# Hybrid MoBA/NSA decoder layer on one core: token projections in 512-column pieces, q and k heads turned in fp32 pairs, weights split up to eight tiles ahead, attention preludes polled in steps

## The chip, the cores and the metric

The kernel runs on one core of one Trainium2 chip. The time is the device time of one execution in microseconds; the runs before agree within 0.2 us. The engines are named as in the profile: PE (TensorE, the matmuls; PEld is its weight load), DVE (VectorE), ACT (ScalarE), POOL (GpSimd) and SP (SyncE, which here issues the DMAs).

## What is computed

One decoder layer on x of 512 tokens by 1024 channels, all in float32. One input projection feeds two mixers: A is a block-sparse attention of 8 heads of 64, B a three-branch attention (compressed, selected, window) of 8 query heads in 2 groups.

```python
h = rms_norm(x, norm_w); proj = h @ w_in            # 1024 -> 5912 columns
(q_a, k_a, v_a, z_a, q_b, kc, vc, ksl, vsl, kwn, vwn, gate_b, z_b, gate_m) = split(proj)
o_a = moba_mixer(rms_norm(q_a), rms_norm(k_a), v_a, bias_a)
o_b = nsa_mixer(rms_norm(q_b), rms_norm(compress(kc)), compress(vc),
                rms_norm(ksl), vsl, rms_norm(kwn), vwn, sigmoid(gate_b), bias_b)
merged = sigmoid(gate_m[:1024]) * ((o_a * silu(z_a)) @ w_branch_a) \
       + sigmoid(gate_m[1024:]) * ((o_b * silu(z_b)) @ w_branch_b)
out = x + merged @ w_out
```

At 512 tokens every block is selected, so both mixers are dense causal attention with a bias: 8 units (one per head) for A, 16 units (a head and a branch) for B.

## The kernel before

**Arithmetic.** Each fp32 operand of a matmul is split into a high and a low part in the reduced type fp32r, and a product is three matmuls: high by high, low by high, high by low (`mm3`; the issuing line of all of them is 343). Weights come from HBM as 128-row tiles of up to 560 columns (`wr`, six buffers), `Stream.split` makes `wh` (a copy on ACT, line 314, or on POOL, line 316) and `wl` (a subtraction on DVE or POOL, line 318). `Stream.take` hands out the next tiles; `ahead` splits at most four tiles ahead of the one in use.

**Projection.** Token-major pieces (`gemm_tok`, PSUM tile `pgt`) compute 128 tokens by n columns: four row tiles t, eight k each, three matmuls per k. The first piece (`gemm_first`, `pgf`) runs k outermost while x arrives. Its columns are 256: `v0`, `v1`, four `qk` pieces with two q heads and two k heads each, `qb0`, `qb1`; `kb` has 280 and `vb` 256. Channel-major pieces (`gemm_chan`, `pgc`) have the weight as the stationary side and all 512 tokens as the moving side: `kc`, `vc`, eight z gates, eight merge gates (`gmgate`).

**From projection to attention.** `norm_split` takes a row tile of four heads out of PSUM (`nraw` on ACT), squares, sums (line 617), takes the power -0.5 on POOL (`nr`, line 385), multiplies (619), applies the gain (614) and splits into high and low halves of a token tile (595, 596). `q_stack` and `k_stack` turn one head, high and low half together, by four 128x128 transposes in fp32r (`stack`, PSUM tile `pq`, line 825) and copy it out (832): `qs`, `ks`, and `kx` with the halves swapped. A unit then makes scores (`sps`, lines 893 and 894), bias and row minimum (912, DVE), exp (927, ACT), the division (931, POOL), the transposes of P in fp32 (`pt`, 940), their split (952 ACT, 954 DVE) and the product with v (`O`, 974).

**Order.** The program is written by a planner at build time. Four generators (x statistics, `attention`, `gemms`, `cmp` for the compression) yield PE work with an assumed cost, or a condition to wait for; the planner picks the generator with the least weighted time whose condition holds, and ACT, DVE and POOL steps hang on chains in a heap of assumed times. So each engine has one fixed order, and every engine runs its order strictly in turn. In `attention` the prelude of unit n+2 (the turns of its head, its bias row `T`) is advanced by one step after each score block of unit n, and what is left of it is run to its end, waits included, before unit n+1. After the last unit `x_again` forms the sums of x (`xa`, `ta`, `tb`, split into `T`, `th`, `hh`, `hl`) that the merge gates of mixer B need. Behind the z and merge gates come the branch products (`pbr`), four `gate_pair`s (`pgw`) and the output projection (`po`).

Of the kernel before, what the change touches and what calls it, by code (L numbers as in the profile page):

```python
# [19 lines left out]
D = 1024  # L20
DH = 64
# [15 lines left out]
NATT = 39  # L37
NW = 8
NRAW = 6
# [36 lines left out]
def tok_layout():  # L76

    lay, n = {}, 0
    for name, cols in tok_pieces().items():
        lay[name] = (n, KT // 2, len(cols))  # L80
        n += KT // 2
    return lay, n
# [3 lines left out]
def hybrid_kernel(ctx: ExitStack, tc: tile.TileContext, x, x0, xT, wtok, wchan, wgate, gains, w1,  # L86
# [28 lines left out]
    RES = {"g": (pg, 2), "s": (pss, 2), "t": (pst, 3), "o": (pso, 1), "sb": (sp, 3), "gmt": (sp, 3), "nraw": (sp, 4),  # L115
# [164 lines left out]
    class Stream:  # L280
# [19 lines left out]
        def split(w, upto):  # L300
            while len(w.chain) < min(upto, len(w.raws)):
# [6 lines left out]
                hi, lo = w.mk_hi()[:, :n], w.mk_lo()[:, :n]  # L308
# [133 lines left out]
    def x_rms():  # L442
# [10 lines left out]
        x_diag(c)  # L453

# [30 lines left out]
    def tok_tiles(name):  # L485
        i0, nt, n = tlay[name]
        return [(wtok[i0 + i][:, :2 * n], 2 * n) for i in range(nt)]
# [4 lines left out]
    ORDER_T = ("v0", "qk0", "qk1", "kc", "qk2", "vc", "v1", "qk3", "qb0", "kb", "vb", "za0", "za1", "qb1", "za2", "za3", "zb0", "zb1", "zb2", "zb3")  # L492
# [41 lines left out]
    for p_, c in [(p_, c) for p_ in (1, 2) for c in range(2)] + [(p_, c) for c in range(2) for p_ in (5, 6, 3, 7, 4)]:  # L534
        tiles += [(operand(p_, 2, 2 * c + i), 512) for i in range(2)]
    W = Stream(tiles, NRAW - 1, lambda: wp.tile([P, WT], F32R, name=nm("wh"), tag="whi"),
               lambda: wp.tile([P, WT], F32R, name=nm("wl"), tag="wlo"))
    W1 = Stream([(w1[kv, q], 512) for kv in range(2) for q in range(8)], 1, lambda: att("vh"), lambda: att("vl"))
# [5 lines left out]
    def gemm_tok(name, emit, tags="gggg"):  # L544
        n = tlay[name][2]
        ws = W.take(4, n)
        for t in range(NT):
            yield room(tags[t])
            ps = psum(tags[t], "pgt")
            hs = [(hh[:, k, t * P:(t + 1) * P], hl[:, k, t * P:(t + 1) * P], None) for k in range(KT)]  # L550
            i = 0
            for c in mm3(ps[:, :n], hs, ws):
                yield c
                if not callable(c):
                    i += 1
                    ahead((t + i / KT) / NT)
            with_rx(lambda t=t, ps=ps: emit(t, ps))

    def gemm_first(name, emit, tags="ggss"):

        n = tlay[name][2]
        ws = W.take(4, n)
        ps = [psum(tag, "pgf") for tag in tags]
        for k in range(KT):
            for a, b in ((0, 0), (1, 0), (0, 1)):
                yield need(f"xl{k}" if a else f"xh{k}")
                if b or not a:
                    yield need((W, b, k // 2))
                for t in range(NT):
                    nc.tensor.matmul(ps[t][:, :n], (hl if a else hh)[:, k, t * P:(t + 1) * P], ws[k][b],  # L570
# [4 lines left out]
            ahead((k + 1) / KT)  # L575

    def gemm_chan(name, emit):
# [5 lines left out]
        for c in mm3(ps, ws, [(hh[:, k, :], hl[:, k, :], None) for k in range(KT)]):  # L583
            yield c
            if not callable(c):
                i += 1
                ahead(i / KT / 2)
# [10 lines left out]
    def norm_split(ch, dst, ps, t, g0):  # L598

        b = {}  # L600

        def f0(e):
            b["raw"] = alloc("nraw", "nraw", (P, 4, DH))
            b["xn"] = sp.tile([P, 4, DH], F32, name=nm("nxn"), tag="nxn", bufs=4)
            b["ss"] = sp.tile([P, 4], F32, name=nm("nss"), tag="nss", bufs=4)
            b["r"] = sp.tile([P, 4], F32, name=nm("nr"), tag="nr", bufs=4)
            e.activation(b["raw"], ps[:, :256].rearrange("p (h d) -> p h d", h=4), AF.Copy, scale=rx[:, t:t + 1])

        def f1(e):
            if g0 == 2:  # L610
                e.tensor_mul(b["xn"], b["xn"], gn[:, g0, :].unsqueeze(1).to_broadcast([P, 4, DH]))
            else:
                x4 = b["xn"].rearrange("p (a b) d -> p a b d", a=2)
                e.tensor_mul(x4, x4, gn[:, g0:g0 + 2, :].unsqueeze(2).to_broadcast([P, 2, 2, DH]))
        ch.do({"A": 358}, f0, ps, "nraw")
        ch.do({"A": ca(256)}, lambda e: e.activation(b["xn"], b["raw"], AF.Square))
        ch.do({"D": cd(256)}, lambda e: e.reduce_sum(b["ss"], b["xn"], axis=AX.X))
        rsqrt_mean(ch, lambda: b["r"], lambda: b["ss"], DH, 4)
        ch.do(either(256), lambda e: e.tensor_mul(b["xn"], b["raw"], b["r"].unsqueeze(2).to_broadcast([P, 4, DH])))
        ch.do(either(256), f1)  # L620
        split(ch, dst, lambda: b["xn"], lambda: b["raw"])
# [7 lines left out]
    def proj_norm(name, g0, tags="gggg"):  # L629
        toks[name] = [None] * NT  # L630

        def emit(t, ps):
            toks[name][t] = att(name)
# [4 lines left out]
            norm_split(ch, hl4(toks[name][t]), ps, t, g0)  # L638
# [8 lines left out]
    def proj_v(name, first=False):  # L647
        toks[name] = [None] * NT

        def emit(t, ps):  # L650
            toks[name][t] = att(name)
            ch = Chain(now[0] + 230)
            dst, src, r = hl4(toks[name][t]), ps[:, :256].rearrange("p (h d) -> p h d", d=DH), rx[:, t:t + 1]
            ch.do({"A": 358}, lambda e: e.activation(dst[:, :, 0, :], src, AF.Copy, scale=r))
            ch.do({"D": 396}, lambda e: e.scalar_tensor_tensor(
                dst[:, :, 1, :], src, r, dst[:, :, 0, :].bitcast(F32), op0=ALU.mult, op1=ALU.subtract), ps)
            ch.mark(f"{name}.{t}")
# [163 lines left out]
    def stack(srcs):  # L821

        pt = psum("t", "pq", F32R)
        for t in range(NT):
            nc.tensor.transpose(pt[:, t * P:(t + 1) * P], srcs[t], identr)  # L825
# [8 lines left out]
    def q_stack(box, srcs):  # L834
        yield room("t")
        pt = stack(srcs)
        yield 4 * 85
        qs = att("qs")
        box.append((qs, Chain(now[0] + 230).do({"A": 478, "D": 600}, lambda e: copy_on(e, qs, pt.bitcast(F32)), pt)))

    def k_stack(box, srcs, first=None):

        yield room("t")
        pt = stack(srcs)
        yield 4 * 85
        ks = att("ks")
        kx = att("kx")
        c = Chain(now[0] + 230)
        c.do({"A": 478, "D": 600}, lambda e: copy_on(e, ks, pt.bitcast(F32)))
        c.do({"A": 478, "D": 600}, lambda e: copy_on(e, kx[0:64, :], pt[64:128, :].bitcast(F32)))  # L850
        c.do({"A": 478, "D": 600}, lambda e: copy_on(e, kx[64:128, :], pt[0:64, :].bitcast(F32)), pt)
        if first is not None:
            for i, z in enumerate((ks, kx)):
                def f(e, dst=first[:, i, :], src=z[:, :P].bitcast(F32)):
# [5 lines left out]
        box.append((ks, kx, c))  # L860
# [159 lines left out]
    def moba_units():  # L1020
        us = []
        for h in range(8):
            p, i = h // 2, h % 2
            box = {"q": [], "k": []}

            def pre(h=h, p=p, i=i, box=box):
                yield toks_of(f"qk{p}")
                yield toks_of(f"v{h // 4}")
                yield from q_stack(box["q"], heads(f"qk{p}", i))
                yield from k_stack(box["k"], heads(f"qk{p}", 2 + i))  # L1030
                yield late
# [572 lines left out]
```

## Time and profile before

| | |
|---|---|
| median of 3 runs | 471.98 us (471.87 to 472.05) |
| the profiled execution | 473.72 us, span of its instructions 471.9 us |
| PE busy | 463.5 us, 98% of the span, 3172 matmuls |
| DVE, ACT, POOL busy | 386.5, 281.1, 184.5 us |
| DMA moved | 74.40 MB, 158 GB/s in the mean |

Rows of a group view read: line, engine, operation, out<-in by the program's names, shape, count | busy us, mean ns of one | idle us of the engine before them and what ended it. A matmul's duration holds its way through the array, which overlaps the next matmul; what it costs the stream is the distance from its start to the next start. In the chain (the work that ended last, followed back) a row is the start, the length, and what ran.

### The profile page before, as it was taken

The page shows a single profiled execution, that of the slowest core. Times are in us where ns is not written, and L with a number is a line of the kernel's source. Part 1 is how long each engine was busy: PE and PEld are TensorE (multiplying, and loading weights), DVE is VectorE, ACT ScalarE, POOL GpSimd, SP SyncE. Part 2 cuts the span into 40 slices and gives each one's busy share as a digit, 9 for nine tenths or more (in the row PEclk, how much of TensorE's full clock was granted, in tenths as well). Part 3 has the DMA queues.
Part 4 walks back from the last instruction along what each step waited for, and adds up shares of the span by engine and source line. Part 5 has one row for each costly group of instructions (what it writes and reads, how often), then busy time and mean ns, then how long its engine had stood idle before and what let it go on. Part 6 is the DMA issues. An engine that isn't in the chain of part 4 may idle for free.

```text
span 471.9 us, 9247 instructions
## 1 busy us (share of the span) xinstructions
PE 463.5 (98%) x3172; PEld 424.2 (90%) x3172; DVE 386.5 (82%) x972; ACT 281.1 (60%) x683; POOL 184.5 (39%) x242
## 2 busy tenths in 40 slices
PE   9999999999999999999999999999998999999997
PEld 9999897999999889888888888888886998999996
DVE  5888899798998569898877967787499699999873
ACT  7667594487776338476777557787473554556220
POOL 0154373048666205445546327555723022202120
PEclk9999999999999999999999999999999999999999
DMA  8925234534334423165565675664996785568862
GB/s 303 269 66 191 58 80 144 149 102 128 108 105 123 116 87 91 48 178 133 160 132 156 141 202 107 179 120 148 261 275 155 264 209 167 163 197 268 248 205 69
DMA packets 41088, 74.40 MB, mean 158 GB/s; under 512 B 3984, under 2 KB 6416, under 8 KB 41040
## 3 DMA queue, kind: packets, MB, share of 16 engines
q1 hardware_dynamic: 32464, 57.02, 39.4%
q0 software_dynamic: 4352, 8.39, 10.9%
q10 hardware_dynamic: 4224, 8.39, 5.3%
q8 instruction: 25, 0.41, 0.4%
q14 instruction: 23, 0.19, 0.1%
HBM read 71.03 MB, written 19.53 MB: 192 GB/s over the span
## 4 chain that ended last, share of the span: by engine, by line
PE 80%; DVE 8%; ACT 5%; POOL 2%; DMA 2%; issue 1%; SPq 0%; POOLq 0%; DVEq 0%; ACTq 0%
PE pgc L343 18%; PE pgt L343 17%; PE pgw L343 9%; PE po L343 8%; PE pbr L343 7%; PE O L974 6%; PE pt L940 5%; PE sps L893 3%; PE sps L894 3%; DVE wl L318 2%; PE pq L825 1%; POOL P L931 1%; DMA wr<-in_w 1%; DMA x<-in_xT 1%; ACT wh L314 1%
## 5 line engine op out<-in xcount | busy, mean ns | idle before, releaser
L318 DVE TENSOR_TENSOR wl<-wr,wh 128x512 fp32r<-128x512 f32 (+1 forms) x139 | 97.3, 714 | 6.5 <-ACT wh L314 5.1
L343 PE MATMUL pgt<-wh,hh 128*128 128x256 f32 (+1 forms) x288 | 82.9, 288 | 1.6 <-DVE X L711 0.8
L343 PE MATMUL pgt<-wl,hh 128*128 128x256 f32 (+1 forms) x288 | 81.5, 283 | 0.3 <-DVE wl L318 0.2
L343 PE MATMUL pgt<-wh,hl 128*128 128x256 f32 (+1 forms) x288 | 81.2, 282 | 0.0
L314 ACT CAST wh<-wr 128x512 fp32r<-128x512 f32 (+1 forms) x98 | 59.1, 615 | 17.2 <-DMA wr<-wsum 11.7
L316 POOL TENSOR_SCALAR wh<-wr 128x512 fp32r<-128x512 f32 (+1 forms) x50 | 39.4, 795 | 76.1 <-DMA wr<-wsum 31.0
L931 POOL TENSOR_SCALAR P<-P,sst,gate 128x512 f32<-128x512 f32 (+3 forms) x56 | 40.3, 728 | 55.4 <-DVE sst L930 42.5
L912 DVE CUSTOM_DVE_ANT_0 sb<-sps,T 128x512 f32<-128x512 f32 (+3 forms) x96 | 46.0, 485 | 18.9 <-PE sps L894 17.7
L343 PE MATMUL pgc<-hh,wh 128*128 128x512 f32 x144 | 59.4, 413 | 0.0
L343 PE MATMUL pgc<-hl,wh 128*128 128x512 f32 x144 | 56.9, 395 | 0.0
L343 PE MATMUL pgc<-hh,wl 128*128 128x512 f32 x144 | 56.8, 395 | 0.0
L927 ACT ACTIVATE P<-sb,sst 128x512 f32<-128x512 f32 (+3 forms) x88 | 50.8, 578 | 9.9 <-DVE sst L912 8.9
L343 PEld LDWEIGHTS pgt<-wh,hh 128*128 128x128 f32 x288 | 54.2, 188 | 2.6 <-PE pgt L343 1.0
L343 PEld LDWEIGHTS pgt<-wl,hh 128*128 128x128 f32 x288 | 54.2, 188 | 0.7 <-DVE wl L318 0.7
L343 PEld LDWEIGHTS pgt<-wh,hl 128*128 128x128 f32 x288 | 54.2, 188 | 0.5
L952 ACT CAST ph<-pt 128x512 fp32r<-128x512 f32 (+2 forms) x72 | 33.2, 478 | 34.9 <-PE pt L940 34.0
L931 POOL TENSOR_SCALAR P<-P,sst 128x512 f32<-128x512 f32 (+3 forms) x32 | 24.8, 779 | 45.4 <-DVE sst L930 38.8
L940 PE MATMUL pt<-cst,P 128*128 128x128 f32 x232 | 40.8, 273 | 0.3 <-POOL P L931 0.2
L954 DVE TENSOR_TENSOR pl<-pt,ph 128x512 fp32r<-128x512 f32 (+2 forms) x72 | 38.4, 549 | 2.1 <-ACT ph L952 1.8
L385 POOL TENSOR_TENSOR nr<-nss,mhalf 128x4 f32<-128x4 f32 x28 | 29.7, 1062 | 24.3 <-DVE nss L384 23.8
L940 PEld LDWEIGHTS pt<-cst,P 128*128 128x128 f32 x232 | 28.9, 140 | 4.8 <-POOL P L931 1.5
L343 PEld LDWEIGHTS pgc<-hl,wh 128*128 128x128 f32 x144 | 27.0, 188 | 6.4
(267 smaller groups left out, 1278.9 us busy)
## 6 DMA issues: line engine op xcount, KB each, us to landing
wr<-in_wtok SPq DMA_DIRECT2D x36, 256.0 KB, 3.0
wr<-wsum SPq DMA_DIRECT2D x32, 256.0 KB, 3.4
wr<-in_wgate SPq DMA_DIRECT2D x28, 256.0 KB, 3.1
wr<-in_wchan SPq DMA_DIRECT2D x20, 256.0 KB, 2.8
T<-rtab SPq DMA_DIRECT2D x16, 256.0 KB, 3.9
wr<-in_w SPq DMA_DIRECT2D x16, 256.0 KB, 2.7
wsum<-in_wgate ACTq DMA_DIRECT2D x4, 1024.0 KB, 5.5
wsum<-wsum POOLq DMA_DIRECT2D x8, 512.0 KB, 6.5
```

The lines of the kernel that those rows point to most:

```text
L314: e.copy(hi, raw)
L316: e.tensor_scalar(hi, raw, 1.0, 1.0, op0=ALU.mult, op1=ALU.mult)
L318: c.do(either(n), lambda e, hi=hi, lo=lo, raw=raw: e.tensor_sub(lo, raw, hi.bitcast(F32))).mark((w, 1, i))
L343: nc.tensor.matmul(dst, sts[i][a], mvs[i][b], start=(start and i == a == b == 0), stop=(stop and i == n - 1 and b == 1), skip_group_check= ...
L385: c.do({"p": 430 + 150 * w}, lambda e: e.tensor_tensor(v(dst), v(ss), mhalf[:parts, :w], op=ALU.pow))
L912: e.tensor_tensor_reduce(z["sb"][:, :L], sps[:, :L], T[:, S - L:], scale=-1.0, scalar=3e38, op0=ALU.add, op1=ALU.min, accum_out=st[:, 0, b ...
L927: e.activation(pv(), z["sb"][:, :L], AF.Exp, bias=st[:, 0, b:b + 1], scale=-1.0, accum_out=st[:, 1, b:b + 1])
L931: c.do({"P": 315 + 0.834 * L}, lambda e: e.tensor_scalar(pv(), pv(), st[:, 2, b:b + 1], g, op0=ALU.mult, op1=ALU.mult))
L940: nc.tensor.transpose(pt[:, (b - kb) * P:(b - kb + 1) * P], u.p0 if u.p0 is not None and b == 0 else u.pb[:, POFF[b] + kb * P:POFF[b] + (k ...
L952: e.copy(z["w"][0], pt[:, :w])
L954: ch.do({"D": cd(w)}, lambda e: e.tensor_sub(z["w"][1], pt[:, :w], z["w"][0].bitcast(F32)), pt)
L974: nc.tensor.matmul(O[0][:, S - n:], v.bitcast(F32) if kb == 3 else v, w, start=(u.first and kb == 0 and i == 0), stop=(u.last and kb == 3 ...
```

## The change

- **Pieces of 512 columns.** `v0` and `v1` become `v`, the four `qk` pieces become two of four q and four k heads, `qb0` and `qb1` become `qb`. A weight tile then holds one k of 512 columns instead of two of 256; there are 40 token tiles as before. `kb` and `vb` keep their columns. `qb` and `kb` change places, and the late `qb1` moves up with `qb0`.
- **Norms on eight heads at a time,** left in fp32: no split of token tiles. The product of the q and the k gain, with the factor 0.125, is formed once in `gn` and applied to k alone, so q gets no gain step.
- **Turns in pairs.** `turn` transposes two fp32 heads at a time (128 columns); `q_pair` copies the high part of each head (ACT) and subtracts for the low part (DVE); `k_pair` writes the high part twice into `ks`, and the low part into both halves of `kx` (DVE, then an ACT copy).
- **Weights further ahead.** `more` splits up to eight tiles ahead during a token piece and during `kc` and `vc`; every second tile of a 512-column piece takes its `wh` and `wl` from the attention pool, which grows from 39 to 41 tiles; `nraw` has two buffers of twice the size.
- **Preludes in steps.** After each score block, the prelude of unit n+1, or of n+2 when that is through, is polled: a step whose condition does not hold yet is put aside. Only before a unit starts is its own prelude run to the end.
- The bias rows and the row of x's scale (`bias_rows`, `x_rows`) move from the GEMM's generator to that of the x statistics, ahead of the second piece.

```diff
-NATT = 39
+NATT = 41
+AHEAD = 8
...
-    d = {f"qk{p}": r(QA + 128 * p, 128) + r(KA_ + 128 * p, 128) for p in range(4)}
-    d.update({f"v{i}": r(VA + 256 * i, 256) for i in range(2)})
-    d.update({f"qb{i}": r(QB + 256 * i, 256) for i in range(2)})
+    d = {f"qk{g}": r(QA + 256 * g, 256) + r(KA_ + 256 * g, 256) for g in range(2)}
+    d.update(v=r(VA, 512), qb=r(QB, 512))
...
-        lay[name] = (n, KT // 2, len(cols))
+        kk = WT // len(cols)
+        lay[name] = (n, KT // kk, len(cols), kk)
...
     def gemm_tok(name, emit, tags="gggg"):
-        n = tlay[name][2]
-        ws = W.take(4, n)
+        _, nt, n, kk = tlay[name]
+        ws = []
         for t in range(NT):
...
+            for k in range(KT):
+                if not t and not k % kk:
+                    ws += W.take(1, n)
+                    W.split(W.i + min(nt - 1 - k // kk, 3))
+                h = hh[:, k, t * P:(t + 1) * P], hl[:, k, t * P:(t + 1) * P], None
+                yield from mm3(ps[:, :n], [h], [ws[k]], start=(k == 0), stop=(k == KT - 1))
+                if t:
+                    f = (t + (k + 1) / KT) / NT
+                    more(int(AHEAD * min(1, f / 0.75) + 0.5), 4 - (k // 2 if t == NT - 1 else 0))
...
-        ch.do({"A": 358}, f0, ps, "nraw")
-        ch.do({"A": ca(256)}, lambda e: e.activation(b["xn"], b["raw"], AF.Square))
-        ch.do({"D": cd(256)}, lambda e: e.reduce_sum(b["ss"], b["xn"], axis=AX.X))
-        rsqrt_mean(ch, lambda: b["r"], lambda: b["ss"], DH, 4)
-        ch.do(either(256), lambda e: e.tensor_mul(b["xn"], b["raw"], ...))
-        ch.do(either(256), f1)
-        split(ch, dst, lambda: b["xn"], lambda: b["raw"])
+        ch.do({"A": 100 + cap(n)}, f0, ps, "nraw")
+        ch.do({"A": ca(n)}, lambda e: e.activation(out, b["raw"], AF.Square))
+        ch.do({"D": cd(n)}, lambda e: e.reduce_sum(b["ss"], out, axis=AX.X))
+        rsqrt_mean(ch, lambda: b["r"], lambda: b["ss"], DH, H)
+        ch.do(either(n), lambda e: e.tensor_mul(out, b["raw"], ...), lambda: b["t"])
...
-            nc.tensor.transpose(pt[:, t * P:(t + 1) * P], srcs[t], identr)
+            nc.tensor.transpose(pt[:, t * P:(t + 1) * P], toks[name][t][:, col:col + P], ident)
...
+        for r, z in enumerate(qs):
+            c.do({"A": 478}, lambda e, r=r, z=z: e.copy(z[0:64, :], pt[64 * r:64 * r + 64, :]))
+        for r, z in enumerate(qs):
+            c.do({"D": 602}, lambda e, r=r, z=z: e.tensor_sub(z[64:128, :], pt[64 * r:64 * r + 64, :], z[0:64, :].bitcast(F32)),
+                 pt if r else None)
...
-                yield from until_cost(nxt, n)
+                for m in range(n + 1, min(n + 3, len(units))):
+                    if m not in over:
+                        yield from poll(m)
+                        break
...
-            yield from nxt
             prev = u
...
     def gemms():
-        yield from proj_v("v0", True)
-        yield from proj_norm("qk0", 0, "ttto")
-        yield from bias_rows()
-        yield from x_rows()
-        yield from proj_norm("qk1", 0)
+        yield from proj_v("v", ("v0", "v1"), True)
+        yield from proj_norm("qk0", 1, "ttto")
         yield from compress_w(0)
-        yield from proj_norm("qk2", 0)
+        yield from proj_norm("qk1", 1)
         yield from compress_w(1)
-        yield from proj_v("v1")
-        yield from proj_norm("qk3", 0)
-        yield from proj_norm("qb0", 2)
         yield from proj_norm("kb", 4)
-        yield from proj_v("vb")
+        yield from proj_norm("qb", 0)
+        yield from proj_v("vb", ("vb",))
```

What the order of the instructions makes of it, at three places. The names carry buffer numbers.

PE at the first preludes, before: the turns of head 0 (`pq_700` q, `pq_708` k) inside the third row tile of the piece `qk1`, behind `v0` and `qk0`. `identr` is the identity in fp32r.

```order
L343 MATMUL pgt_665<-wl_483,hh 128x256
L825 MATMUL pq_700<-identr,qk_455 128x128
L825 MATMUL pq_700<-identr,qk_457 128x128
L825 MATMUL pq_700<-identr,qk_511 128x128
L825 MATMUL pq_700<-identr,qk_557 128x128
L825 MATMUL pq_708<-identr,qk_455 128x128
L825 MATMUL pq_708<-identr,qk_457 128x128
L825 MATMUL pq_708<-identr,qk_511 128x128
L825 MATMUL pq_708<-identr,qk_557 128x128
L825 MATMUL pq_719<-identr,qk_455 128x128
```

The same place on PE now; `cst` is the fp32 identity.

```order
L344 MATMUL pgt_707<-wl_517,hh 128x512
L850 MATMUL pq_715<-cst,qk_503 128x128
L850 MATMUL pq_715<-cst,qk_565 128x128
L850 MATMUL pq_715<-cst,qk_616 128x128
L850 MATMUL pq_715<-cst,qk_659 128x128
L850 MATMUL pq_725<-cst,qk_503 128x128
L850 MATMUL pq_725<-cst,qk_565 128x128
L850 MATMUL pq_725<-cst,qk_616 128x128
L850 MATMUL pq_725<-cst,qk_659 128x128
L344 MATMUL pgt_707<-wh_531,hh 128x512
```

What were two stacks for one head (a third, `pq_719`, begins the next head) are two stacks for two heads. They stand inside the first row tile of the new `qk1`, behind `v`, the whole of the new `qk0` (four q and four k heads) and `kc`.

DVE at the norms of `qk0`, before: the steps of several 256-column row tiles, with the split of the finished ones (line 596).

```order
L619 TENSOR_TENSOR nxn_468<-nraw_467,nr_470 128x256
L617 TENSOR_REDUCE nss_565<-nxn_564 128x4
L614 TENSOR_TENSOR nxn_468<-nxn_468,gn 128x256
L384 TENSOR_SCALAR nss_565<-nss_565 128x4
L619 TENSOR_TENSOR nxn_473<-nraw_472,nr_475 128x256
L318 TENSOR_TENSOR wl_586<-wr_399,wh_585 128x512
L614 TENSOR_TENSOR nxn_473<-nxn_473,gn 128x256
L596 TENSOR_TENSOR qk_455<-nxn_468,qk_455 128x4x64
L619 TENSOR_TENSOR nxn_518<-nraw_517,nr_520 128x256
```

The same place on DVE now: four steps per row tile of eight heads, with weight splits of the next pieces between them.

```order
L636 TENSOR_REDUCE nss_509<-qk_503 128x8
L385 TENSOR_SCALAR nss_509<-nss_509 128x8
L319 TENSOR_TENSOR wl_554<-wr_498,wh_553 128x512
L638 TENSOR_TENSOR qk_503<-nraw_508,nr_510 128x512
L641 TENSOR_TENSOR qk_503<-qk_503,gn 128x256
L319 TENSOR_TENSOR wl_578<-wr_537,wh_577 128x512
L636 TENSOR_REDUCE nss_573<-qk_565 128x8
L385 TENSOR_SCALAR nss_573<-nss_573 128x8
L319 TENSOR_TENSOR wl_596<-wr_540,wh_595 128x512
```

The split is gone. Of the multiplications the one with the power (638) now covers eight heads, and the one with the gain (641) the 256 k columns of those alone.

DVE at the end of attention, before: `ys` takes over the last attention output, `gm_5049` is the last merge gate of the first half, and the sums of x (`ta`, `tb`) stand behind it, between the branch products (line 1347).

```order
L1003 TENSOR_TENSOR ys_4938<-O_5011,ot_5132 64x512
L318 TENSOR_TENSOR wl_5135<-wr_4795,wh_5134 128x512
L1013 TENSOR_TENSOR ys_4938<-ys_4938,zs_3843 128x512
L1206 TENSOR_TENSOR gm_5049<-pgc_5050,R 128x512
L1015 TENSOR_TENSOR yl_5146<-ys_4938,yh_5145 128x512
L1214 TENSOR_TENSOR ta_5105<-xa_5101 128x256
L318 TENSOR_TENSOR wl_5167<-wr_4841,wh_5166 128x512
L1215 TENSOR_TENSOR ta_5105<-xa_5103,ta_5105 128x256
L1347 SCALAR_TENSOR_TENSOR gm_4001<-gm_4001,pbr_5154 128x512
L1214 TENSOR_TENSOR ta_5111<-xa_5107 128x256
```

The same place on DVE now: `gm_4364` is the third last merge gate.

```order
L1037 TENSOR_TENSOR ys_4174<-O_4249,ot_4369 64x512
L319 TENSOR_TENSOR wl_4373<-wr_4019,wh_4372 128x512
L1047 TENSOR_TENSOR ys_4174<-ys_4174,zs_3464 128x512
L1049 TENSOR_TENSOR yl_4385<-ys_4174,yh_4384 128x512
L319 TENSOR_TENSOR wl_4399<-wr_4105,wh_4398 128x512
L1256 TENSOR_TENSOR ta_4340<-xa_4336 128x256
L1257 TENSOR_TENSOR ta_4340<-xa_4338,ta_4340 128x256
L1248 TENSOR_TENSOR gm_4364<-pgc_4365,R 128x512
L1256 TENSOR_TENSOR ta_4346<-xa_4342 128x256
L1268 SCALAR_TENSOR_TENSOR T_4335<-ta_4340,T_4335 128x256
```

Attention now ends three whole merge-gate products (72 matmuls of 512 columns on PE) before the branch products, where it ended in the last of them (12 matmuls before its end), and three quarters of the sums of x are made beside those products.

More of the change, by code (lines that the diff above doesn't have):

```diff
@@ L453, in x_rms @@
         x_diag(c)
+        yield from bias_rows()
+        yield from x_rows()
     def x_diag(c):
@@ L549, in gemm_tok, with more @@
             ps = psum(tags[t], "pgt")
[L550 to L556, printed above, removed]
-            with_rx(lambda t=t, ps=ps: emit(t, ps))
+            for k in range(KT):
[7 more added lines that the diff above has]
+                    more(int(AHEAD * min(1, f / 0.75) + 0.5), 4 - (k // 2 if t == NT - 1 else 0))
+            with_rx(lambda t=t, ps=ps: emit(t, ps))
+    tlay_next = ("kc", "vc")
+    def more(n, used):
+        i = W.i
+        while i < W.i + n:
+            used += i not in from_att
+            if used > NW:
+                break
+            i += 1
+        W.split(i)
     def gemm_first(name, emit, tags="ggss"):
         n = tlay[name][2]
-        ws = W.take(4, n)
         ps = [psum(tag, "pgf") for tag in tags]
         for k in range(KT):
+            w = W.take(1, n)[0]
+            W.split(W.i + 2) if k < 5 else more(k, 4)
             for a, b in ((0, 0), (1, 0), (0, 1)):
@@ L574, in gemm_first @@
                 yield cm(n) * NT
-            ahead((k + 1) / KT)
+        W.split(W.i + 4)
     def gemm_chan(name, emit):
@@ L586, in gemm_chan @@
                 i += 1
-                ahead(i / KT / 2)
+                if name in tlay_next:
+                    more(int(8 * min(1, i / KT) + 0.5), 2)
+                else:
+                    ahead(i / KT / 2)
         emit(ps)
@@ L1094, in pre0 @@
             box["pcc"] = cc
-            yield late
             yield room("T")
@@ L1145, in attention, with drain, poll @@
         pres = [p() for p, _ in units]
-        yield from pres[0]
-        yield from pres[1]
-        prev = None
-        def until_cost(g, n):
-            if n in lates:
-                return
-            for v in g:
-                if v is late:
-                    lates.add(n)
-                    return
-                yield v
-                if not callable(v):
-                    return
-        lates = set()
+        pend, over = {}, set()
+        def drain(m):
+            if m in pend:
+                yield pend.pop(m)
+            yield from pres[m]
+            over.add(m)
+        def poll(m):
+            while True:
+                v = pend.pop(m, None) or next(pres[m], None)
+                if v is None:
+                    over.add(m)
+                    return
+                if not callable(v):
+                    yield v
+                    return
+                t = v()
+                if t is None or t > now[0]:
+                    pend[m] = v
+                    return
+        prev = None
         for n in range(len(units) + 1):
             u = units[n][1] if n < len(units) else None
-            nxt = pres[n + 2] if n + 2 < len(units) else iter(())
             if u:
+                yield from drain(n)
                 yield from u.start()
```

177 lines of the change are left out of this document (95 added, 82 removed).

## The prediction

> **What bounds the kernel now.** I read first the busy table of the page and its row of the granted clock, then the shares of the chain, PE's waits, and PE beside the other engines in three stretches. "DVE" is the third group of the second row.
>
> ```profile
> span 471.9 us, 9247 instructions
> PE 463.5 (98%) x3172; PEld 424.2 (90%) x3172; DVE 386.5 (82%) x972; ACT 281.1 (60%) x683; POOL 184.5 (39%) x242
> PEclk9999999999999999999999999999999999999999
> PE 80%; DVE 8%; ACT 5%; POOL 2%; DMA 2%; issue 1%; SPq 0%; POOLq 0%; DVEq 0%; ACTq 0%
> ```
>
> PE is busy for 98% of the span at the full granted clock, and 80% of the chain runs on it. So there are two ways to gain: less work in PE's stream, and fewer holes in it. The holes that have a releaser:
>
> ```profile
> PE pbr L343 <- ACT hh L1228: 1.4, 1, 1.4
> PE pw L402 <- POOL ones L357: 0.9, 1, 0.9
> PE pgt L343 <- DVE X L711: 0.8, 1, 0.8
> PE pgt L343 <- ACT nraw L607: 0.7, 1, 0.7
> PE hps L740 <- DVE vl L318: 0.3, 1, 0.3
> PE pt L940 <- POOL P L931: 0.2, 1, 0.2
> PE pgt L343 <- DVE wl L318: 0.2, 1, 0.2
> ```
>
> Their sum is 4.5 us, 0.9 of it the start of the program. So at most 3.6 us is to be had from these waits; the rest of a gain must come from PE's own work. The second engine is DVE. In windows, with columns span; then busy (and count) of PE, PEld, DVE, ACT, POOL; clock; DMA share; GB/s:
>
> ```profile
> 60.00:70.00 10.00, 10.00 (x79) 9.61 (x78) 9.69 (x32) 9.55 (x27) 7.11 (x9) 1.00 0.24 51
> 200.00:240.00 40.00, 39.77 (x229) 34.17 (x228) 33.83 (x106) 26.96 (x76) 19.12 (x28) 1.00 0.62 158
> 340.00:366.00 26.00, 24.65 (x107) 19.65 (x106) 25.23 (x44) 14.13 (x29) 7.71 (x7) 1.00 0.81 217
> ```
>
> DVE is 97% busy from 60 to 70 us and from 340 to 366 us, 85% in the attention between. In the first PE loses nothing, in the last it does. The 1.4 us wait lies there:
>
> ```profile
> 360.47 1.51 DVE L1218 TENSOR_TENSOR tb<-ta,xa 128x256 f32<-128x256 f32 x1
> 362.07 0.62 ACT L1228 CAST T<-tb 128x512 fp32r<-128x512 f32 x1 [5.14 <-DVE tb L1218]
> 363.06 0.47 PE L343 MATMUL pbr<-yh,wh 128*128 128x512 f32 x1 [1.35 <-ACT hh L1228]
> ```
>
> The sums of x that end attention run on DVE beside the branch products, and ACT, waiting 5.14 us for one of them (`tb`), is late with the casts that stand ahead of what PE needs.
>
> **The change, part by part.**
>
> *Pieces of 512 columns.* What one matmul costs PE's stream is read from unbroken stretches of the chain:
>
> ```profile
> 148.91 4.27 PE pgt L343 x36
> 266.57 8.34 PE pgc L343 x36
> ```
>
> 36 matmuls of 256 columns take 4.27 us, 118.6 ns each; 36 of 512 take 8.34 us, 231.7 ns each. A pair of the former is 237.2 ns, so a merge saves 5.5 ns. How many there are (the others of these three parts have the same count):
>
> ```profile
> L343 PE MATMUL pgt<-wh,hh 128*128 128x256 f32 x256 | 73.4, 287 | 1.6 <-DVE X L711 0.8 <-ACT nraw L607 0.7
> L570 PE MATMUL pgf<-wh,hh 128*128 128x256 f32 x32 | 5.8, 306 | 0.0
> ```
>
> 3 x (256 + 32) = 864, of which the 96 of `vb` keep their width. 768 x 118.6 ns = 91.1 us become 384 x 231.7 ns = 89.0 us: **-2.1 us**, all of it on PE's path.
>
> The Trainium skill, page "TensorE: Matmul & The Clock Gate", section "Back-to-back issue gap", puts an isolated warm matmul of N columns at N/2.4 + 2.5 ns, a fixed part of 2.5 ns per matmul; by that the 384 merges would give 1.0 us where the rows give 2.1. Its 109.2 and 215.8 ns lie under the measured 118.6 and 231.7, so here the measurement decides.
>
> *Turns in pairs.* The transposes now:
>
> ```profile
> L825 PE MATMUL pq<-identr,qk x64: 220/245/306, 39.1 to 135.3; 128*128 128x128 f32 x64
> L825 PE MATMUL pq<-identr,qb x32: 224/246/304, 180.2 to 260.1; 128*128 128x128 f32 x32
> L825 PE MATMUL pq<-identr,kb x16: 221/246/304, 174.7 to 254.9; 128*128 128x128 f32 x16
> ```
>
> 112 in fp32r, 28 stacks of four; after, 14 stacks of four in fp32. No fp32 `pq` exists before; the nearest row is `pt`, the transposes of P, fp32 against the same identity. Both kinds in the stream, each with the matmuls behind it:
>
> ```profile
> 40.90 0.46 PE L825 MATMUL pq<-identr,qk 128*128 128x128 f32 x4
> 41.20 0.35 PE L343 MATMUL pgt<-wh,hh 128*128 128x256 f32 x1
> 41.38 0.28 PE L343 MATMUL pgt<-wh,hl 128*128 128x256 f32 x1
> ...
> 130.01 0.60 PE L940 MATMUL pt<-cst,P 128*128 128x128 f32 x4
> 130.36 0.38 PE L343 MATMUL pgt<-wh,hh 128*128 128x280 f32 x1
> 130.58 0.30 PE L343 MATMUL pgt<-wh,hl 128*128 128x280 f32 x1
> ```
>
> From the stack's start to the second matmul behind it is 0.48 us in fp32r; less 0.12 for the matmul between, 0.36 us. In fp32 it is 0.57 less 0.13 (280 columns at the rate of 118.6 ns for 256), 0.44; other `pt` stacks lie a little above, so I take 0.45. 28 x 0.36 = 10.1 us become 14 x 0.45 = 6.3 us: **-3.8 us**. The ends: at 0.36 a stack -5.0, at twice the fp32r price -0.
>
> *Norms of eight heads, no split, halves made behind the turn.* This is work of DVE and ACT. DVE's rows, the last one of a size that it gets now:
>
> ```profile
> L617 DVE TENSOR_REDUCE nss<-nxn 128x4 f32<-128x256 f32 x28 | 11.4, 410 | 0.1
> L619 DVE TENSOR_TENSOR nxn<-nraw,nr 128x256 f32<-128x256 f32 x24 | 12.0, 498 | 2.1 <-POOL nr L385 1.8
> L596 DVE TENSOR_TENSOR qk<-nxn,qk 128x256 fp32r<-128x256 f32 x13 | 5.8, 445 | 1.7 <-ACT qk L595 1.7
> L384 DVE TENSOR_SCALAR nss<-nss 128x4 f32<-128x4 f32 x28 | 5.4, 196 | 0.1
> L614 DVE TENSOR_TENSOR nxn<-nxn,gn 128x256 f32<-128x256 f32 x17 | 7.5, 442 | 0.1
> L832 DVE CAST kx<-pq 64x512 fp32r<-64x512 f32 x7 | 4.8, 687 | 0.6 <-ACT ks L832 0.3
> L1003 DVE TENSOR_TENSOR ys<-O,ot 64x512 f32<-64x512 f32 x16 | 10.9, 680 | 3.6 <-ACT ot L999 3.4
> ```
>
> By the order, DVE's part of the token splits (23 x 0.445 = 10.2 us) goes. Of the sums, 28 x 0.41 = 11.5 become 12 of twice the width, estimated at the 0.68 of `ys`, and 4 of the old: 9.8. Of the products, 24 x 0.498 = 12.0 become 11 x 0.68 + 4 x 0.498 = 9.5. New are 28 subtractions behind the turns, 28 x 0.68 = 19.0; gone are 15 copies of the old turns at the 0.687 of `kx`, 10.3, 11 of 17 gain steps, 4.9, and 12 of 28 small scalings of 0.196, 2.4. Together DVE loses some 13 us of 386. None of it is on PE's path as long as DVE keeps its lead, so I book it at nothing; the cover is the GEMM that stands between a head's turn and its first score. With that cover gone, each of the 14 pairs would hold PE by at least its two subtractions, 1.4 us, 19 us in all.
>
> *Order.* The first score now stands here:
>
> ```profile
> 43.04 0.40 PE L893 MATMUL sps<-ks,qs 128*128 128x512 f32 x1
> ```
>
> In the new order 252 matmuls of 512 columns and two stacks stand ahead of it behind the start at 5.5 us: 5.5 + 58.4 + 0.9 = 65 us. Attention begins 22 us later. It nevertheless ends earlier against the rest: behind its last PE work stood 12 matmuls of 512 columns (2.8 us) ahead of the branch products, now 72 (16.7 us). So the sums of x have 14 us more until PE needs their successors, and the wait of 1.4 us (`pbr`) goes: **-1.4 us**. The two waits of `pgt` (0.8 and 0.7) belong to pieces that no longer exist. Their kind stays: a row tile of a token piece has to be copied out before its PSUM buffer serves again. With 512 columns the row tile's matmuls last 24 x 231.7 ns = 5.6 us, so the copies have twice the time; but in `kb`, of 280 columns, two tiles are reused in a tight row behind a 512-column piece. I put 1.5 us back for such waits, as much as goes: 0.
>
> *Weights.* A tile of the new pieces serves one k, three matmuls of 512, 0.695 us, where a tile of two k served six of 256, 0.71 us, in the first row tile of a piece; in the other three no tile is needed. The pace asked of DVE at a piece's head is so the same, and what eight tiles of lead give is cover for the head. No gain, no loss; the ends are the 0.2 us of the `wl` wait going, and a hole at some of the six heads, up to 0.7 us each, the time of one tile, 4 us. The bias and x rows are moved, with the same instructions on PE: three matmuls, booked at 0; they now stand among GEMM of the first pieces. SP issues the same 222 DMAs; the bias row's comes earlier and attention's later, so no queue gets more to carry before its first user.
>
> *Sum:* -2.1 - 3.8 - 1.4 = -7.3, and with the tenths of the smaller waits -7.4 us. The profiled execution took 473.72 us, 1.74 above the median of the runs, so the difference is set against the median: 471.98 - 7.4 = **464.6 us**. What a measurement of this kernel can tell is about 0.2%, 0.9 us.
>
> **The rivals.**
>
> *The PE work goes, the waits eat part of it.* The work alone, 5.9 us, gives 466.1. If in addition the heads of the six pieces each cost up to 0.7 us (4 us) and the reuse in `kb` another, it is 470 to 471. For it: DVE at 97% where pieces follow each other (60 to 70 us), and every prelude put off makes a later lump. Against it: in that very stretch PE lost nothing. 466 to 471, **0.30**.
>
> *Slower: attention starved.* The 24 units now have to fit between 65 us and the end of attention, with fewer GEMM matmuls between their blocks. If PE, as it waits on the chain of minimum, exp and division, loses 0.3 us per unit, 24 x 0.3 = 7.2 us eat the gain; that is the point from which it decides. At 0.5 us it is 12 us and 476.6. For it: DVE is at 85% between 200 and 240 us, and the same chains pack closer. Against it: PE's wait for `P` was 0.2 us in all, and DVE has 13 us less. **0.07**.
>
> *More than that.* If every wait of the list but the start's goes, -5.9 - 3.6 = -9.5, 462.5; DVE's 13 us may also close the small holes that no row of the list names, a few us more, to 460. **0.08**.
>
> *Nothing comes of it.* The merges bring less per matmul than the rows of an unbroken stretch say, fp32 stacks cost near twice, and 1.4 us moves elsewhere: within 0.2% of before, **0.05**.
>
> *PE's rate at 512 columns.* If long streams of 512 columns ran at 131 ns each, as PE's weight path and array overlapped, the 384 merged ones would take 50 us in place of 91: 40 us less, 431. The row of 36 `pgc` at 231.7 ns says that they do not; under **0.01**. The Trainium skill states that rate, in the same section, as the sustained spacing of matmuls of 512; no stretch of this trace shows it.
>
> **How the numbers follow.** The forecast of 464.6, own range 462.5 to 466, has 0.50, then 0.30 for 466 to 471, 0.08 below, 0.05 for none and 0.07 for slower. From 461.0 to 470.0 lie 0.50, some 0.25 of the second and 0.06 of the third. Faster by over 0.2% are the first three, 0.88.
>
> **What would show it.** In the profile after: 2694 matmuls of the program beside the warm-up, token pieces at 232 ns from start to start, 56 `pq` rows of fp32 whose stacks cost about 0.45 us; DVE near 373 us; no wait of `pbr` on ACT; first score near 65 us. I am wrong if PE's list has new rows of over 2 us in sum (`pgt` on `wl` at the heads, `sps` on `qs` or `ks`, `pt` on `P`), if the `pq` stacks cost much over 0.45 us, or if the tail behind the branch products, which the change does not touch, gets longer because its weights come at another time.

## The result, and the profile after

| | before | after |
|---|---|---|
| median of the runs beside the first profile | 471.93 us (4 runs) | 465.98 us (4 runs, 464.87 to 466.52) |
| median of the runs in the second comparison | 472.97 us (11 runs) | 465.68 us (4 runs, 465.25 to 466.57) |
| span of the profiled executions | 471.9 and 473.0 us | 464.7 and 464.8 us |

The ratio of after to before is 0.9874 (95% interval 0.9851 to 0.9898) in the first comparison and 0.9848 (0.9827 to 0.9868) in the second: faster by 6 to 7 us (5.95 and 7.29 by the medians). The forecast was 464.6 us, a gain of 7.4; the spans fell by 7.2 and 8.2 us.

The page of after, the span and the busy time of the engines:

```profile
span 464.7 us, 8250 instructions
PE 456.1 (98%) x2732; PEld 399.2 (86%) x2732; DVE 373.4 (80%) x902; ACT 281.7 (61%) x654; POOL 178.9 (38%) x227
```

PE is busy for 7.4 us less and for the same share of the span. DVE has lost 13.1 us (386.5 to 373.4), as estimated. The waits of PE after:

```profile
PE hps L766 <- DVE vl L319: 2.0, 3, 1.4
PE pw L403 <- POOL ones L358: 0.9, 1, 0.9
PE pkt L816 <- DVE kh L812: 0.6, 1, 0.6
PE pk L799 <- DVE gt L785: 0.5, 1, 0.5
PE po L344 <- ACT wh L315: 0.5, 1, 0.5
PE sps L927 <- DVE sst L946: 0.2, 1, 0.2
PE pt L974 <- DVE pl L988: 0.2, 1, 0.2
```

Their sum is 4.9 us where it was 4.5: not one of the old waits of the pieces and of the branch product (`pgt`, `pbr`) is left, and three stand in the compression, which multiplies its 16 key and value weights (`vh`, `vl`) in `hps` and then works through `pk` and `pkt`. That of `hps` has grown from 0.3 to 2.0 us, the other two are new. The stretches of after (span; busy and count of PE, PEld, DVE, ACT, POOL; clock; DMA share; GB/s):

```profile
40.00:80.00 40.00, 40.00 (x191) 32.92 (x191) 29.99 (x67) 24.09 (x48) 20.15 (x19) 1.00 0.35 103
80.00:140.00 60.00, 56.72 (x355) 49.36 (x354) 53.74 (x145) 47.80 (x121) 34.81 (x42) 1.00 0.32 98
180.00:340.00 160.00, 159.76 (x879) 135.98 (x878) 130.97 (x373) 105.92 (x279) 71.92 (x99) 1.00 0.60 153
320.00:345.00 25.00, 25.00 (x109) 20.04 (x108) 22.90 (x44) 17.46 (x35) 5.95 (x6) 1.00 0.80 230
```

PE is now without a hole from 40 to 80 us and in the stretch at the end of attention; 3.3 us are missing from 80 to 140 us, where DVE is 90% busy. Before, the row of the same 60 us had no hole; the hole lay ahead of them, 1.8 us between 40 and 80 us:

```profile
40.00:80.00 40.00, 38.23 (x267) 34.76 (x265) 36.66 (x99) 28.80 (x70) 19.80 (x26) 1.00 0.34 93
80.00:140.00 60.00, 60.00 (x484) 58.66 (x485) 52.41 (x143) 42.15 (x113) 30.26 (x38) 1.00 0.43 122
```

Where PE's time went, by groups: for each matmul the distance from its start to the start of the next one, summed in the profiled executions (467.2 us from the first start to the last before, 460.0 after).

| group | before | after | difference |
|---|---|---|---|
| token pieces (`pgf`, `pgt`) | 119.7 | 116.0 | -3.7 |
| turns (`pq`) | 8.8 | 5.1 | -3.7 |
| branch, gate and output products (`pbr`, `pgw`, `po`) | 126.1 | 124.7 | -1.4 |
| scores (`sps`) | 34.5 | 33.4 | -1.1 |
| compression (`hps`) | 8.7 | 10.8 | +2.1 |
| channel-major pieces (`pgc`) and `pt` | 122.6 | 123.6 | +1.0 |
| all others | 46.8 | 46.4 | -0.4 |

A wait counts with the group of the matmul that started ahead of it, and what a stack of transposes adds to the matmul behind it counts with that matmul.

### The profile page after: what moved, and what is told of

Same layout as the page of the kernel before. It is cut to its first block, busy times and chain, and to the rows that moved or that the text cites. A ratio compares the mean times of both kernels' runs of the same rounds, so it can differ in the third digit from the quotient of the medians.

```text
span 464.7 us, 8250 instructions
## 1 busy us (share of the span) xinstructions
PE 456.1 (98%) x2732; PEld 399.2 (86%) x2732; DVE 373.4 (80%) x902; ACT 281.7 (61%) x654; POOL 178.9 (38%) x227
## 4 chain that ended last, share of the span: by engine, by line
PE 76%; DVE 12%; ACT 4%; issue 3%; DMA 2%; POOL 2%; SPq 0%; ACTq 0%; DVEq 0%; POOLq 0%
PE pgc L344 18%; PE pgt L344 12%; PE pbr L344 10%; PE pgw L344 9%; PE pgf L593 5%; PE po L344 5%; PE O L1008 5%; PE pt L974 4%; PE sps L927 2%; PE sps L928 2%; DVE wl L319 2%; DVE sb L946 2%; DMA wr<-wsum 1%; DVE pl L988 1%; DMA wr<-in_w 1%
## 5 line engine op out<-in xcount | busy, mean ns | idle before, releaser
L315 ACT CAST wh<-wr 128x512 fp32r<-128x512 f32 (+1 forms) x105 | 62.9, 618 | 29.0 <-DMA wr<-wsum 7.1
L317 POOL TENSOR_SCALAR wh<-wr 128x512 fp32r<-128x512 f32 x43 | 34.7, 814 | 76.2 <-DMA wr<-wsum 14.8
L344 PE MATMUL pgt<-wh,hh 128*128 128x512 f32 (+2 forms) x160 | 57.3, 358 | 0.0
L344 PE MATMUL pgt<-wh,hl 128*128 128x512 f32 (+2 forms) x160 | 56.3, 352 | 0.0
L344 PE MATMUL pgt<-wl,hh 128*128 128x512 f32 (+2 forms) x160 | 56.3, 352 | 0.0
L344 PEld LDWEIGHTS pgt<-wl,hh 128*128 128x128 f32 x160 | 30.1, 188 | 4.3
L386 POOL TENSOR_TENSOR nr<-nss,mhalf 128x8 f32<-128x8 f32 (+1 forms) x16 | 26.1, 1633 | 19.6 <-DVE nss L385 19.1
L344 PEld LDWEIGHTS pgt<-wh,hl 128*128 128x128 f32 x160 | 30.2, 189 | 3.4
L344 PEld LDWEIGHTS pgt<-wh,hh 128*128 128x128 f32 x160 | 30.1, 188 | 3.4
L344 PE MATMUL po<-wh,mh 128*128 128x256 f32 x112 | 31.5, 282 | 0.5 <-ACT wh L315 0.5
```

Of the source, the lines that this page charges most:

```text
L315: e.copy(hi, raw)
L317: e.tensor_scalar(hi, raw, 1.0, 1.0, op0=ALU.mult, op1=ALU.mult)
L344: nc.tensor.matmul(dst, sts[i][a], mvs[i][b], start=(start and i == a == b == 0), stop=(stop and i == n - 1 and b == 1), skip_group_check= ...
L386: c.do({"p": 430 + 150 * w}, lambda e: e.tensor_tensor(v(dst), v(ss), mhalf[:parts, :w], op=ALU.pow))
```

## The experiments

Their kernels are told of by the parts that they change; times are medians, each beside runs of the kernel before on the same chip, and "after" is 465.68 us unless said otherwise. The medians of before beside them lie between 472.45 and 473.11 us, and after itself stands in one of these comparisons alone, so a difference to after of under 1 us says nothing by itself.

**The two kernels again.** No edit.

> The changed kernel once more, unaltered, beside the kernel before, to narrow the interval. If the difference of the profiled executions is the true one (467.25 to 460.01 us from the first matmul's start to the last's, 7.2 us), the difference of the medians comes out at 7.2 us, 464.8 against 472.0. If the difference of the medians first seen (471.93 to 465.98) is the true one, it is 5.9 us and the profile of before was of a long execution by some 1.3 us.

> The kernel before, unaltered, for a second profile. If the first one (span 471.9 us, 473.72 us in all) was of a long execution, this one has a span near 470.2 us and some of its waits (0.7 and 0.8 us of the row tiles, 1.4 us of the branch product) come out smaller. If not, the span is 471.9 us again.

After: 465.68 us against 472.97, 7.3 us. The kernel before: 474.75 us, span 473.0 us. So the first profile of before was not of an unusually long execution: runs of the kernel before reach from 470.89 to 475.27 us over all comparisons, much further than the 0.2 us within which the first three agreed. In this second profile of before the wait of `pbr` on ACT is missing, and two of 0.9 us each stand in its place, `pgw` on DVE and on ACT, in the same stage.

**Each 512-column matmul as two of 256.**

```diff
-    yield from mm3(ps[:, :n], [h], [ws[k]], ...)
+    for a, b in ((0, 0), (1, 0), (0, 1)):
+        for z in (slice(0, 256), slice(256, 512)):
+            nc.tensor.matmul(ps[:, z], h[a], ws[k][b][:, z], ...)
```

(and the same in `gemm_first`.)

> The changed kernel with each matmul of 512 columns of its token pieces issued as two of 256 columns, in the same order; all else unaltered. If the rows of the unbroken stretches are right (231.7 ns against 2 x 118.6 ns), the 384 pairs cost 5.5 ns each more, +2.1 us: 468.1 us. If a matmul has a fixed part of only 2.5 ns, +1.0 us: 467.0 us. If a long stream of 512 columns ran much faster than two of 256, tens of us more.

466.50 us (ratio to before 0.986, 0.9836 to 0.9884), 0.8 more than after, not clear of the noise. The chain has the price itself, the same stretch of `qk0` in after:

```profile
29.71 22.40 PE pgt L344 x96
```

and in the split kernel:

```profile
30.33 22.62 PE pgt L567 x192
```

22.40/96 = 233.3 ns for one of 512, 2 x 22.62/192 = 235.6 ns for two of 256: 2.3 ns a merge, 0.9 us for 384. Summed from start to start over all of them it is 92.2 against 91.0 us, 1.2. The merges are worth about 1 us, not 2.1. This is the size that the Trainium skill gives, page "TensorE: Matmul & The Clock Gate", section "Back-to-back issue gap": a fixed part of 2.5 ns in each isolated matmul, beside a streaming part. The difference agrees. What the section's formula gives for 512 columns, an estimate of 215.8 ns, stays below the 233.3 ns measured here, and its sustained 131 ns is seen in no run here.

**Each pair turn transposed twice.**

```diff
-        for t in range(NT):
+        for t in list(range(NT)) * 2:
             nc.tensor.transpose(pt[:, t * P:(t + 1) * P], toks[name][t][:, col:col + P], ident)
```

> The changed kernel with each of the 14 pair turns transposed twice into the same PSUM tile, 56 transposes more; all else unaltered. If a stack of four in fp32 costs PE 0.45 us as the prediction took it, +6.3 us: 472.3 us, and the saving of 3.8 us from 28 stacks of 0.36 to 14 of 0.45 holds. If part of a stack is hidden under the matmuls around it, a second one behind the first costs its plain 0.35 us or so: +4.9 us. If the later copies make PE wait, over 7 us.

469.62 us (0.9934, 0.9914 to 0.9953), +3.9. The chain of this kernel, two turns with each stack doubled:

```profile
59.08 1.75 PE pq L850 x16
```

1.75/4 = 0.44 us for a stack of four. From start to start `pq` takes 11.2 us instead of 5.1, +6.1. So the price of 0.45 holds, and yet the time rises by 3.9: the waits behind shrink as PE comes later, those of `hps` from 2.0 to 1.1, and `pk`'s 0.5 is gone. A PE that waits for DVE pays for its own extra work only in part.

**The steps of the compression placed later.** The planner writes a waiting step where its assumed time says that the input is ready; here it waits another 1.5 us (`hps`) or 1.0 us (`pk`, `pkt`).

```diff
+    def later(f, d):
+        def g():
+            t = f()
+            return None if t is None else t + d
+        return g
...
-                yield ws[i][2].ready
+                yield later(ws[i][2].ready, 1500)
...
-        yield ch.ready
+        yield later(ch.ready, 1000)
```

> The changed kernel with a later place in the order for three steps of the compression: a step that waits for a weight half, for the activation or for the normed key is written 1.5 or 1.0 us after the assumed time instead of at it. PE's new waits there are 2.0 (hps on vl), 0.6 and 0.5 us. If they are new waits that the changed order made, of work that PE could do meanwhile, most of 3.1 us goes: 462.6 to 463.7 us against 465.7. If PE is held there by DVE's load, they return behind other names and nothing is won: 465.7 us.

462.75 us (0.9791, 0.9769 to 0.9813), 2.9 less than after: the fastest of all, 9.7 us under its runs of before (472.45). The waits of its PE, all of them:

```profile
PE pw L403 <- POOL ones L358: 0.9, 1, 0.9
PE scp L1105 <- DVE sc L1111: 0.4, 1, 0.4
PE sps L934 <- DVE sst L953: 0.2, 1, 0.2
```

The three waits are gone, and under another name only 0.4 us came (`scp`). In the stretch of the compression PE now misses 0.25 us instead of 3.3, although DVE is as busy there as in after, 91%:

```profile
80.00:140.00 60.00, 59.75 (x374) 52.71 (x373) 54.68 (x154) 47.63 (x121) 37.19 (x45) 1.00 0.39 114
```

Over the whole run DVE is busy for 4.8 us less than in after (368.6), most of it behind 340 us, where the new order falls out differently too; whether that has a part in the 2.9 us is not shown.

The longest of the three in after, seen on DVE, POOL and PE (rows of the timeline):

```profile
112.96 0.96 DVE L638 TENSOR_TENSOR kb<-nraw,nr 128x256 f32<-128x256 f32 x1 [0.26 <-POOL nr L386]
113.28 0.28 PE L765 MATMUL hps<-vh,xs 128*128 128x256 f32 x1
113.61 0.79 POOL L317 TENSOR_SCALAR wh<-wr 128x512 fp32r<-128x512 f32 x1
113.84 1.09 DVE L319 TENSOR_TENSOR vl<-wr,vh 128x512 fp32r<-128x512 f32 x1
114.48 1.59 POOL L319 TENSOR_TENSOR wl<-wr,wh 128x512 fp32r<-128x512 f32 x1
114.99 0.39 PE L766 MATMUL hps<-vl,xs 128*128 128x256 f32 x1 [1.43 <-DVE vl L319]
```

PE has the high half `vh`; the low half is behind a product of the `kb` norm on DVE, and both run long beside POOL's work (0.96 and 1.09 us where products of that shape took 0.50 and splits of 512 columns 0.71 in the mean before). Of the `wl` splits of 512 columns on DVE in after, 6 of the 40 that overlap work of POOL take over 0.85 us and none of the other 95; what sets the 6 apart is not shown. PE has other work in its list, but behind the wait.

**Preludes with their waits.**

```diff
-                for m in range(n + 1, min(n + 3, len(units))):
-                    if m not in over:
-                        yield from poll(m)
-                        break
+                if n + 1 < len(units):
+                    yield from step(n + 1)      # one step, its waits included
```

> The changed kernel with the preludes not put aside: after each score block the prelude of the next unit is run one step further, with the waits that it meets, as the old rule did (one unit ahead, since the paired heads leave no tiles for two). The order then ends attention behind the first branch products. If the early end of attention is what took away the wait of the branch product (1.4 us), it comes back: 467 us or more against 465.7. If DVE's lighter load took it away, the time stays within 0.9 us of 465.7.

467.28 us (0.9882, 0.9855 to 0.991; runs from 464.88 to 469.13), +1.6, with an interval that overlaps after's. The place is shown, the size is not: attention ends behind the first branch products again, and a wait of 1.4 us is back in that stage.

```profile
PE pgw L344 <- DVE hl L1275: 1.4, 1, 1.4
PE hps L766 <- POOL vl L319: 1.4, 1, 1.4
```

**Four tiles of lead.**

```diff
-AHEAD = 8
+AHEAD = 4
-    tlay_next = ("kc", "vc")
+    tlay_next = ()
```

> The changed kernel with weights split at most four tiles ahead, in the token pieces and in kc and vc. As booked in the prediction the eight tiles of lead are cover for the heads of the pieces: without it a piece's head of eight tiles at 0.70 us each meets DVE's 0.71 us a tile, and loses between 0 and 4 us: 465.7 to 470, most likely about 1 us. If the lead does nothing, 465.7.

467.75 us (0.99, 0.9876 to 0.9924), +2.1 (by the two ratios of after 1.2 to 2.5). The token pieces take 118.1 us from start to start instead of 116.0, those of 512 columns behind the first one 71.1 instead of 68.4, and their heads wait for weights:

```profile
PE pgt L344 <- DVE wl L319: 1.0, 2, 0.8
```

**Sums of squares twice.** Once with the planner not knowing it, in after's order; then in the kernel with the later compression, told; and in the kernel before.

```diff
-        ch.do({"D": cd(n)}, lambda e: e.reduce_sum(b["ss"], out, axis=AX.X))
+        def sums(e):
+            for _ in range(2):
+                e.reduce_sum(b["ss"], out, axis=AX.X)
+        ch.do({"D": cd(n)}, sums)               # told: 2 * cd(n)
```

> The changed kernel with the sum of squares of each normed row tile formed twice: 12 x 0.68 + 4 x 0.41 = 9.8 us more work on DVE in the same order, most of the 13 us that the change took off it. If that relief is worth nothing to PE, as booked, 465.7 us. If DVE's lateness is what PE meets in this stretch (the compression's waits of 3.1 us), a part of 9.8 us shows: 467 to 470 us.

471.54 us (0.9975, 0.9962 to 0.9989), +5.9; DVE is busy for 9.5 us more (382.9). Two windows of this kernel, and the largest waits in them:

```profile
80.00:140.00 60.00, 55.31 (x349) 48.19 (x349) 55.34 (x147) 45.19 (x116) 34.48 (x42) 1.00 0.34 98
140.00:180.00 40.00, 37.95 (x241) 32.92 (x240) 34.28 (x80) 31.55 (x68) 22.32 (x27) 1.00 0.37 108
```

```profile
PE hps L769 <- DVE vl L319: 2.1, 2, 1.8
PE pt L977 <- POOL P L968: 1.6, 2, 1.1
PE pq L853 <- DVE kx L886: 1.0, 1, 1.0
```

DVE is 92% busy from 80 to 140 us, and PE misses 4.7 us there instead of 3.3; from 140 to 180 us it misses 2.1 us instead of the 0.1 of after:

```profile
140.00:180.00 40.00, 39.86 (x271) 36.13 (x269) 32.55 (x82) 30.39 (x67) 22.05 (x26) 1.00 0.37 112
```

The waits lie where a unit's prelude, its softmax and the compression meet, most of them for work that does not come out of the norms (`vl`, `P`): DVE runs its order in turn, and what stands behind the longer sums is late too.

PE has the same order in both kernels, so each matmul can be set against itself. This kernel is 0.1 us behind after at 70 us, 2.1 at 90, 2.5 at 130 and 4.8 from 175 us on; the last doubled sum stands at 169 us, and from there to 420 us nothing more is lost. So the four doubled sums ahead of the first score (38 to 54 us, 2.7 us of DVE work) cost nothing, and the other 7.1 us cost 4.8: 0.6 us for each us is a mean.

> The kernel before, with the sum of squares of each of its 28 normed row tiles formed twice: 28 x 0.41 = 11.5 us more on DVE, in the same order. In the changed kernel 9.8 us more cost 5.9 us, 0.6 us for each. If the kernel before was as sensitive, it takes about 6.9 us more, 479 us, and the 13 us that the change takes off DVE were worth much to it by themselves. If only the changed order is sensitive (its attention starts later and packs closer), the kernel before gives 0 to 2 us more, 472 to 474.5 us.

480.04 us against 473.11 (1.0152, 1.0125 to 1.0178), +6.9, or 5.9 to 8.4 by the interval, as the first theory gave: about 0.6 us for each us of DVE work. The kernel before was as sensitive. The four largest waits of its PE:

```profile
PE pq L828 <- DVE qs L835: 1.4, 1, 1.4
PE pw L402 <- POOL ones L357: 0.9, 1, 0.9
PE sps L897 <- DVE kx L835: 0.9, 1, 0.9
PE pgt L343 <- DVE X L714: 0.9, 1, 0.9
```

The last of them was there already (0.8). Set matmul by matmul against before, in whose order it runs, this kernel is 0.2 us behind at 40 us, just ahead of the first score, 6.7 at 105, still 6.7 at 153 and 7.8 at 192. So the first 14 doubled sums, 5.7 us of work, cost 6.5 us, the next eight nothing, the last six 1.1. The price is not one rate, but depends on the place.

> The kernel with the later steps of the compression (462.75 us) and the same 9.8 us of doubled sums on DVE that cost the changed kernel 5.9 us, but now with their cost told to the planner, which can place the waiting steps later. If the loss comes from an order that does not know of the load, most of it goes: within 2 us of 462.75. If DVE's time itself is what is short in this stretch, 4 to 6 us remain: 467 to 469 us.

467.39 us (0.9876, 0.9852 to 0.99), 4.6 more than 462.75, 4.0 by the two ratios. Told of the load, the planner saves little of the 5.9: from 80 to 140 us DVE is now busy for 55.9 us, 93%, and PE misses 3.4 us, where it missed 0.25 with DVE at 91%. So DVE's time itself is short in this stretch. A load of the same size at another place of DVE's order was not tried.

**The bias and x rows put back.**

```diff
-        yield from bias_rows()                  # list of the x statistics
-        yield from x_rows()
...
         yield from proj_norm("qk0", 1, "ttto")
+        yield from bias_rows()
+        yield from x_rows()
```

> The changed kernel with the bias rows and the row of x's scale formed behind qk0 in the projection's own list, where they stood before, and not in the list of the x statistics. The prediction booked this part of the change at nothing: within 0.9 us of 465.7. If the early bias rows are what lets the preludes go on in time, it is slower by 1 us or more; if their three matmuls ahead of the second piece hold PE, faster.

466.38 us (0.9857, 0.9831 to 0.9883), +0.7: no difference that can be told, as booked.

**More slack everywhere.**

```diff
-LAT = 60
+LAT = 160
```

> The kernel with the later steps of the compression, and in addition 160 ns instead of 60 assumed between the end of any step and its use, so that every waiting step is written somewhat later. If waits of under 0.1 us all over the order still hold PE (about 7 us of such small holes stand in the attention of the changed kernel's trace), part of them goes: 459 to 462 us. If PE's small holes are the cost of the matmuls themselves, no change: 462.75 us; if the order gets too loose, attention ends later and it is slower.

463.73 us (0.9796, 0.9773 to 0.982) against 462.75: no gain. With this slack nothing is to be had beyond the compression; other values were not tried.

## Why the prediction was right

The time of 465.98 (465.68) lies in the range, at the upper end of the forecast's own one and next to the 466.1 from which the rival "the PE work goes, the waits eat part of it" counts. The time does not tell the two apart. In the trace the named waits did not shrink as the forecast had it (4.5 to 4.9 us), and the new ones exceed the 2 us that the prediction gave as a sign of being wrong. That the sum came out is in part luck: merges worth 1 us less than booked and new waits of about 3 us were balanced by some 2.5 us of waits and holes in the pieces, which the prediction had put back, and by smaller gains that it did not book.

- **Merges, -2.1.** Too large. The step took the price of 512 columns from the channel-major `pgc` (231.7 ns); the merged token pieces run at 233.3 ns, and the split kernel puts the merges at about -1 us.
- **Turns, -3.8.** Right: -3.7 from start to start, and 0.44 us for a stack.
- **Matmuls.** 2688 stand beside the 44 of the warm-up, as the prediction's own terms give (3172 - 44 - 384 - 56); its 2694 is a slip in the sum.
- **End of attention, -1.4.** Right in size: the three products behind it took 1.4 us less, and in the kernel with waiting preludes, whose attention ends late, a wait of that size is back. DVE is about as light there (375.8 us) as in after (373.4), so its lighter load alone does not take the wait away. An early end under the old load was not tried.
- **Waits of the token pieces, "as much as goes: 0".** Wrong. The pieces lost 3.7 us and the merges account for 1 to 1.2 of it; the other 2.5 us or so are waits and small holes that went, and no wait was found where they were to return, the reuse in `kb`. With four tiles of lead some 2 us of them are back, so the lead has a part in it.
- **New waits.** That rival expected up to 5 us of them at the heads of the pieces and in `kb`. They came, 3.1 us, but in the compression, a place the prediction did not name, since none of its code was changed. Only its neighbours on DVE and POOL in the order had. Moving those steps later gives 2.9 us back, about what their rows say; the planner's whole order shifts with it, so the three were not priced one by one.
- **Weights eight tiles ahead, booked at nothing.** As cover they were worth about 2 us, inside the ends given (0 to 4 us).
- **DVE's 13 us, booked at nothing.** This step fails. "As long as DVE keeps its lead" was taken as given because PE lost nothing at 97% DVE in one stretch. But 9.8 us put back on DVE cost 5.9 us, and 11.5 us cost the kernel before 6.9; in that very stretch, 60 to 70 us, the loaded kernel before falls back by 2.1 us. The lead was there in places: the four sums ahead of after's first score and eight between 105 and 153 us of before cost nothing. With most of the relief taken back, the whole change was worth 0.25% (ratio 0.9975). So the 5 us of PE work (1 of the merges, 3.7 of the turns) alone do not carry the gain; without the relief as much comes back in waits. It is not the new order that makes DVE count, since the kernel before paid about the same 0.6 us. How large the relief's own share is stays open: work put on DVE is not the mirror image of work taken off, and the relief was not tried alone in the kernel before. The rival of a starved attention had the right mechanism, PE waiting for DVE's part of a chain, but the loss of 0.3 us per unit from which it decides is not there: the units' own waits in after's list are 0.2 us (`sps`) and 0.2 us (`pt`) in all, and the stretch from 180 to 340 us misses 0.24 us.

The first score stands at 66.15 us in the profile after, where 65 was counted.

```profile
66.15 0.40 PE L927 MATMUL sps<-ks,qs 128*128 128x512 f32 x1
```

## What to carry to other kernels

Put a doubled cheap operation on the second engine before you book its relief at nothing: here a bound engine that is 98% busy paid 0.6 us in the mean for each us on another that is 80% busy in the mean, both in one fixed order. Then look where it pays, by setting each instruction against itself: in some stretches nothing, in others the whole of the added time. When an order is replanned, look for new waits in the parts that were not changed, since their neighbours were; and try to write a step that waits for a loaded engine a microsecond later than its input is assumed ready, if there is other work to put ahead, as the compression's steps did here. Take a price from the very kind of operation that will run, and check it by undoing that part alone.

## What the runs showed of the hardware

- At a granted clock of 1.00 matmuls of 512 columns follow each other at 233.3 ns in the token pieces and two of 256 at 235.6 ns: the width gains 2.3 ns a merge, about 1%.
- A stack of four fp32 transposes of 128 columns costs 0.44 us when it stands behind another one. Between matmuls it is the same: in after the next matmul starts 0.35 us behind the stack's start (100.22 us) and itself takes 0.20 us to the next start, where 256 columns otherwise take 0.12.
- DVE at 80% in the mean did not have 20% to spare: it was at 90% from 80 to 140 us in after, and work added there held PE. The Trainium skill, page "Perfetto Trace Analysis", section "Optimizing Scalar/DVE Operations", says that the scalar and vector engines can cause bubbles on others without being saturated; the trace agrees: DVE at 80% of after's span, and 0.6 us of time in the mean for each us added.
